# A two-layer decoder trunk in float32: the MLP's down projection as Strassen products

## The chip, the cores and the metric

The kernel runs on one core of a Trainium2 chip. The metric is the device time of one execution in microseconds (us). Times are medians of several executions. The engines of a core work side by side, each through its own queue in order: TensorE (matmuls; PE in the profile, its weight loads PEld), VectorE (DVE), ScalarE (ACT), GpSimd (POOL) and SyncE (SP, which issues most DMAs).

## The reference

`x` is [1, 256, 2048] in float32: 256 tokens. Two layers follow each other. Each has a mixer (several kinds of attention between an input and an output projection) and an MLP; the change touches the MLP. In float32:

```python
def squared_relu_mlp(h, w_up, w_down):
    return jnp.square(jax.nn.relu(h @ w_up)) @ w_down

for layer in range(2):
    ...
    h = rms_norm(x, mlp_norm[layer])
    x = x + squared_relu_mlp(h, w_up[layer], w_down[layer])
return rms_norm(x, final_norm)
```

`w_up` is [2048, 8192] and `w_down` [8192, 2048] for each layer.

## The kernel before

**Three passes.** A float32 product is made of three matmul passes in the type float32r. Weights and activations are split into a high and a low part, w = wh + wl and x = xh + xl, and wh·xh + wh·xl + wl·xh is summed in PSUM. Activations lie feature-major; a moving operand is the tile [xh | xl] of 512 columns.

**The weight stream.** All projections form one list, `stream`, of (block, chunk). A `Block` is 256 output columns of a projection; a `Chunk` is four K-tiles of it (4 x 128 rows x 256 columns). A `Unit` is one load, usually 4 K-tiles x 512 columns (1 MB), which serves one chunk of each of two blocks (`pair` weaves the two). The main loop goes through the list. For chunk i it issues, in this order: ScalarE's copy of the high part (`hi_to`, line 1077) up to chunk i+4; VectorE's subtraction for the low part (`lo_to`, line 1085) up to chunk i+3; the matmuls of chunk i (`consume`); and then `jobs.tick()`. There are three raw buffers, five for hi and four for lo. A raw buffer is loaded anew once the last chunk of its load has its low part.

**The kinds of a block.** "T" (lines 445 to 448): for each K-tile and each of two column tiles, a matmul of the high weights over 512 columns [xh | xl] and one of the low weights over 256 columns (xh). "N" (lines 434 to 436): the activations are stationary and the weights move, three matmuls of 256 columns. "last" (lines 440 to 442): three matmuls of 256 columns with the weights stationary; only the last 256 columns of the last layer are of this kind.

**Side work.** Norms, splits and attention are generators in `Jobs`. `tick` runs those that are due; a `yield d, pe` puts the next step off by d ticks. What a step issues stands in the engines' queues behind what the loop has issued by then.

**The MLP.** The hidden 8192 columns go in two groups of 4096. For each group the up projection runs (16 blocks of 16 K-tiles), its results are squared and split into h (`up_done`, lines 933 to 946), and then the down projection over these 4096 rows (8 blocks of 32 K-tiles), whose results are scaled by the norm and added to the residual xT (`down_done`). The order of the blocks is written out by hand.

Of the kernel before, what the change touches and what calls it, by code (L numbers as in the profile page):

```python
# [38 lines left out]
class Jobs:  # L39
    """Side work (attention, norms, splits) that is woven between the weight chunks."""  # L40
# [48 lines left out]
class Ring:  # L89
    """Order of use of the buffers of one tag: a buffer is free once its key is done."""  # L90
# [13 lines left out]
class Unit:  # L104
    """One load: up to 4 K-tiles x 512 columns of a weight, for one or two chunks."""
# [5 lines left out]
class Chunk:  # L111
    """Some K-tiles of a block: views(raw) are the parts of the load in the order of the operand."""

    def __init__(self, unit, kts, views):
        self.unit, self.kts, self.views = unit, kts, views
        unit.users += 1


class Block:
    """256 output columns of one projection (128 where tiles is 1)."""  # L120

    def __init__(self, kind, chunks, mov, done, tiles=2):
        self.kind, self.chunks, self.mov, self.done, self.tiles = kind, chunks, mov, done, tiles
        self.total = sum(len(c.kts) for c in chunks)
        self.count, self.ps = 0, None
# [3 lines left out]
def trunk(ctx, tc, x, attn_norm, mlp_norm, w_up, w_down, ev_w_in, ev_q_norm, ev_w_uq, ev_kv_norm,  # L129
# [5 lines left out]
    psum = ctx.enter_context(tc.tile_pool(name="psum", bufs=1, space=bass.MemoryType.PSUM))  # L135
    ctx.enter_context(tc.manual_schedule())
# [48 lines left out]
    # the tensor engine's clock rises while the first loads are under way  # L185
    def keep_warm(n):
        if "warm" not in st:
            st["warm"] = psum.tile([P, 2, 512], F32, name="mm", bufs=3)[:, 0]
# [22 lines left out]
    def make_xs(b, g0):  # L211
        """Next phase's moving operand from residual block b, and its sum of squares."""
# [19 lines left out]
    def sum_squares(acc, ms, size):  # L232
        """ms [P, 2] <- mean square + eps per token, tokens on partitions."""
# [5 lines left out]
    def broadcast(r, rB):  # L239
        """rB [P, T] <- r [P, 2] along the free axis, on every partition."""  # L240
# [46 lines left out]
    def w_chunks(w, c0, groups, width=512):  # L287
        """Loads of K-tile groups x width columns of w [K, N]: the chunks of each 256 columns."""
# [23 lines left out]
    def evac(ps, dst, scale=None, rB=None):  # L312
        """dst [P, 2, T] <- sum of the bank halves, times scale, times rB along tokens."""
# [11 lines left out]
    def scores(pairs, dist, cs, u):  # L325
        """u [P, 2, 384] <- biased logits of two heads: [q0 k0 | q1 k0 | q1 k1]."""
# [9 lines left out]
    def neg_max(u, nm):  # L336
        """nm [P, 2 (q tile), 2 (head)] <- -max."""
# [13 lines left out]
    def transpose_p(u):  # L351
        """In place: [k0 q0 | k0 q1 | k1 q1]."""
# [55 lines left out]
    stream = []  # L408

# [4 lines left out]
    def consume(block, i, hi, lo):  # L414
        if block.ps is None:
            block.ps = psum.tile([P, 2, 512], F32, name="mm", bufs=3)
            if block.kind == "last":
                block.ps = [block.ps[:, 0, 0:T], psum.tile([P, 2, 512], F32, name="mm", bufs=3)[:, 0, 0:T]]
# [9 lines left out]
        for n, j in order:  # L428
# [10 lines left out]
            if block.kind == "last":  # L439
# [14 lines left out]
    def even_mixer():  # L454
# [5 lines left out]
        def open_pool():  # L460
            pool = E["pool"] = pool_ctx.enter_context(tc.tile_pool(name="even", bufs=1, reuse_waits="tile"))
# [78 lines left out]
        # the shared rotary key, on both partition halves  # L540
# [11 lines left out]
        def rotate(src, n, outs):  # L552
            """outs <- src*cos + swap(src)*sin; src [P, n, T]."""
# [29 lines left out]
        # per-head projections  # L583
# [38 lines left out]
        def cut(view, pr, width, a, b):  # L622
            """The columns a:b of the two heads, width columns each, of a load."""
# [68 lines left out]
        # output projection  # L692
# [18 lines left out]
    def odd_mixer():  # L711
# [7 lines left out]
        def open_pool():  # L719
            pool = E["pool"] = pool_ctx.enter_context(tc.tile_pool(name="odd", bufs=1, reuse_waits="tile"))  # L720
# [78 lines left out]
        # dilated groups: slots 2*sp, 2*sp+1 of the three groups, one joint softmax  # L799
# [112 lines left out]
    def mlp(layer, last):  # L912
# [6 lines left out]
        def open_pool():  # L919
# [316 lines left out]
```

## Time and profile before

| | us |
|---|---|
| median of 3 runs | 2188.74 (2188.19 to 2188.99) |
| span of the profiled execution, first to last instruction | 2186.0 |
| TensorE busy | 2173.6 |
| VectorE busy | 1298.6 |
| ScalarE busy | 1022.6 |

The span is counted from the first to the last instruction of one profiled execution. Its whole time has 2 to 3 us around the span, as the runs show beside it. Busy times of TensorE overlap, since a matmul begins before the one ahead has drained; prices are read from one start to the next.

### The profile page before, as it was taken

The numbers are of one execution on the slowest core, as the hardware profiler recorded it, in microseconds if no ns is written. First come the engines' busy times: TensorE is split into PE (matmuls) and PEld (weight loads), VectorE is DVE, ScalarE is ACT, GpSimd is POOL, SyncE is SP. The second block draws the span as 40 slices with busy tenths as digits, with TensorE's granted clock in tenths as the row PEclk, the third lists the DMA queues.
The fourth block names the chain that finished last, engine by engine and source line by source line (L and its number), as shares of the span: only waits on it lengthen the run. The fifth ranks groups of instructions, "written<-read, shape, count | busy, mean of one in ns | idle before, by whom it ended". The sixth has DMA issues, their size and how long they took to land.

```text
span 2186.0 us, 31244 instructions
## 1 busy us (share of the span) xinstructions
PE 2173.6 (99%) x12902; PEld 1917.1 (88%) x12902; DVE 1298.6 (59%) x1576; ACT 1022.6 (47%) x1377; POOL 12.8 (1%) x24
## 2 busy tenths in 40 slices
PE   9999999999999999999999999999999999999998
PEld 7898988888888888888888889988888888888887
DVE  6766666656545565556667665566565556655554
ACT  6554544444434444444445446444443334444443
POOL 0000000000000000000000000000000000000000
PEclk9999999999999999999999999999999999999999
DMA  8544455555555555655654456665555555555544
GB/s 260 182 149 155 147 188 184 184 194 175 198 187 192 191 182 187 207 190 176 188 166 148 154 174 190 158 193 184 186 183 199 185 184 189 192 185 183 191 154 135
DMA packets 211374, 396.26 MB, mean 181 GB/s; under 512 B 8904, under 2 KB 31504, under 8 KB 211104
## 3 DMA queue, kind: packets, MB, share of 16 engines
q1 hardware_dynamic: 210720, 392.33, 55.3%
q8 instruction: 101, 1.65, 0.3%
q0 software_dynamic: 480, 1.94, 0.3%
q14 instruction: 41, 0.34, 0.0%
q10 hardware_dynamic: 32, 0.01, 0.0%
HBM read 392.15 MB, written 2.10 MB: 180 GB/s over the span
## 4 chain that ended last, share of the span: by engine, by line
PE 99%; DMA 0%; ACT 0%; SPq 0%; DVE 0%; POOLq 0%; issue 0%; ACTq 0%; DVEq 0%
PE mm L445 55%; PE mm L446 30%; PE mm L448 3%; PE mm L435 2%; PE mm L434 2%; PE mm L436 2%; PE side L333 1%; PE side L356 1%; PE side L402 1%; PE side L331 1%; PE mm L442 0%; PE mm L440 0%; PE mm L441 0%; PE side L403 0%; DMA latqs<-ev_w_in 0%; PE side L873 0%
## 5 line engine op out<-in xcount | busy, mean ns | idle before, releaser
L1085 DVE TENSOR_TENSOR lo<-raw,hi 128x1024 fp32r<-128x1024 f32 (+1 forms) x756 | 898.6, 1194 | 627.2 <-PE mm L446 555.4
L1077 ACT ACTIVATE hi<-raw 128x1024 fp32r<-128x1024 f32 (+1 forms) x756 | 780.6, 1036 | 804.9 <-PE mm L445 712.4
L445 PE MATMUL mm<-xs,hi 128*128 128x512 f32 x2805 | 995.3, 396 | 0.5 <-ACT hi L1077 0.3
L446 PE MATMUL mm<-xs,lo 128*128 128x256 f32 x2992 | 820.5, 279 | 0.2 <-DVE lo L1085 0.2
L445 PE MATMUL mm<-h,hi 128*128 128x512 f32 x1922 | 675.0, 393 | 0.0
L445 PEld LDWEIGHTS mm<-xs,hi 128*128 128x128 f32 x2805 | 526.0, 188 | 121.1 <-ACT hi L1077 1.0
L446 PEld LDWEIGHTS mm<-xs,lo 128*128 128x128 f32 x2992 | 561.4, 188 | 8.8 <-DVE lo L1085 0.5
L446 PE MATMUL mm<-h,lo 128*128 128x256 f32 x1984 | 548.7, 279 | 0.0
L445 PEld LDWEIGHTS mm<-h,hi 128*128 128x128 f32 x1922 | 360.2, 187 | 84.4
L446 PEld LDWEIGHTS mm<-h,lo 128*128 128x128 f32 x1984 | 371.9, 187 | 2.8
L434 PE MATMUL mm<-hi,xs 128*128 128x256 f32 x320 | 91.8, 287 | 0.0
L936 DVE TENSOR_TENSOR t<-mm,t 128x512 f32<-128x512 f32 x64 | 44.3, 691 | 77.3 <-ACT t L935 77.3
L436 PE MATMUL mm<-hi,xs 128*128 128x256 f32 x320 | 89.7, 280 | 0.0
L435 PE MATMUL mm<-lo,xs 128*128 128x256 f32 x320 | 89.7, 280 | 0.0
L935 ACT ACTIVATE t<-mm 128x512 f32<-128x512 f32 x64 | 38.3, 598 | 100.3 <-PE mm L448 100.3
L448 PE MATMUL mm<-xs,hi 128*128 128x512 f32 x187 | 69.9, 396 | 0.0
L445 PE MATMUL mm<-oT,hi 128*128 128x512 f32 x192 | 67.6, 394 | 0.0
L435 PEld LDWEIGHTS mm<-lo,xs 128*128 128x128 f32 x320 | 60.3, 188 | 0.2
L434 PEld LDWEIGHTS mm<-hi,xs 128*128 128x128 f32 x320 | 60.3, 188 | 0.2
L436 PEld LDWEIGHTS mm<-hi,xs 128*128 128x128 f32 x320 | 60.2, 188 | 0.0
L446 PE MATMUL mm<-oT,lo 128*128 128x256 f32 x192 | 53.6, 279 | 0.0
L315 ACT ACTIVATE t<-mm 128x512 f32<-128x512 f32 x37 | 22.1, 598 | 53.8 <-PE mm L448 53.8
(266 smaller groups left out, 1494.3 us busy)
## 6 DMA issues: line engine op xcount, KB each, us to landing
raw<-w_up SPq DMA_DIRECT2D x128, 1024.0 KB, 5.3
raw<-w_down SPq DMA_DIRECT2D x120, 1024.0 KB, 5.0
raw<-od_w_in SPq DMA_DIRECT2D x36, 1024.0 KB, 5.1
raw<-ev_w_in SPq DMA_DIRECT2D x30, 1024.0 KB, 5.4
raw<-ev_w_out SPq DMA_DIRECT2D x16, 1024.0 KB, 5.0
raw<-od_w_in SPq DMA_DIRECT2D x20, 512.0 KB, 4.1
raw<-od_w_out SPq DMA_DIRECT2D x16, 512.0 KB, 6.0
raw<-w_down SPq DMA_DIRECT2D x16, 512.0 KB, 3.6
```

Of the source, the lines that this page charges most:

```text
L315: act(t, ps[:, :, T:], AF.Copy, scale=1.0 if scale is None else scale)
L331: mm(ps[:, 0:P], q[:, 0:P], k[:, 0:P], start=(i == 0), stop=(i == n - 1))
L434: mm(o, xh, hi[:, n], start=first, stop=False)
L435: mm(o, xh, lo[:, n], start=False, stop=False)
L436: mm(o, xl, hi[:, n], start=False, stop=last)
L445: mm(ps[:, j], hi[:, n, c], m, start=first, stop=False)
L446: mm(ps[:, j, 0:T], lo[:, n, c], m[:, 0:T], start=False, stop=False)
L448: mm(ps[:, j], hi[:, n, c], m, start=False, stop=True)
L935: act(t, ps[:, :, T:], AF.Copy)
L936: tt(t, ps[:, :, 0:T], t, op=OP.add)
L1077: act(d, r, AF.Copy)
L1085: tt(d, r, f32(h), op=OP.subtract)
```

## The change

The MLP's hidden columns go in eight groups of 1024. The first seven groups' down projection is made of Strassen products (the form with seven products, and sums shared between them). A 2 x 2 block here is two token halves (128 tokens) by two K-tiles on the activations' side, and two K-tiles by two halves of 512 columns on the weights' side. The activations are stationary (seven combinations of 128 tokens, high and low part), the weights move (256 columns).

- `up_done` evacuates with a relu and a square on ScalarE; its job makes four sums on VectorE and the seven combinations, split into high and low, in `hs` (eight buffers of seven combinations).
- The weights of one load give four chunks: products 1 and 2 (unchanged weights), 3 (unchanged), 5 and 7 (a first set of differences, `prep13`), 6 and 4 (a second set, `prep24`). VectorE makes the differences, ahead of the hi copies.
- The seven product sums of a column block of 512 lie in PSUM tiles s0 and s1 (two banks each) over one group. ScalarE copies them to a stage tile, and a POOL DMA adds them to a DRAM tensor (the first group writes it).
- Behind the seventh group `combine` reads the seven sums back, adds them on VectorE, scales by the norm on ScalarE, and transposes on TensorE into the residual.
- The products of a group are woven with the up projection of the next: two product chunks, one up chunk. Up blocks are of the new kind "U" (three matmuls of 256 columns, both passes of the high weights into the same PSUM columns), one bank each, two buffers. Up loads and the last group's down loads are 8 K-tiles x 256 columns.
- The last group's down projection stays "T" (and "last"), over 8 K-tiles. A residual block is finished once `combine` and this block have both added to it.
- PSUM tiles for blocks come from a pool that each phase opens anew. Comments are taken out; the lines stay in place.

```diff
+        mm(ps[:, j], hi[:, n, c], m[:, 0:T], ...)      # kind "U"
+        mm(ps[:, j], hi[:, n, c], m[:, T:], ...)
+        mm(ps[:, j], lo[:, n, c], m[:, 0:T], ...)
...
+    def consume_products(block, i, hi, lo):
+        chunk = block.chunks[i]
...
+        for o, (a, prod) in enumerate(chunk.prods):
+            half, at = HOME[prod]
+            if half not in block.ps:
+                block.ps[half] = banks(half, 1)
+            ps = block.ps[half].rearrange("p b c -> p (b c)")[:, at * T:(at + 1) * T]
+            for q, pr in enumerate(chunk.kts):
+                x = block.mov(pr)
+                first, last = block.count < 4 and q == 0, block.count >= block.total - 4 and q == 1
+                mm(ps, x[:, a, 0:P], hi[:, o, q], start=first and at % 2 == 0, stop=False)
+                mm(ps, x[:, a, 0:P], lo[:, o, q], start=False, stop=False)
+                mm(ps, x[:, a, P:], hi[:, o, q], start=False, stop=last and (at % 2 == 1 or prod == 3))
+        block.count += 1
+        if block.count == block.total - 2:
+            block.done("s0", block.ps["s0"])
+        if block.count == block.total:
+            block.done("s1", block.ps["s1"])
...
-        NGRP = 2
+        NGRP = 8
...
         def up_done(grp, b):
             def f(ps):
-                r = E["pool"].tile([P, 2, T], F32, name="hr", bufs=3)
                 t = temp()
-                act(t, ps[:, :, T:], AF.Copy)
-                tt(t, ps[:, :, 0:T], t, op=OP.add)
-                stt(r, t, 0.0, t, op0=OP.max, op1=OP.mult)
+                act(t, ps, AF.Relu)
+                r = E["pool"].tile([P, 8, P], F32, name="hr", bufs=1)
+                act(r[:, 0:4].rearrange("p (j k) t -> p j (k t)", j=2), t, AF.Square)
 
                 def job():
-                    h = hs[grp, b] = E["pool"].tile([P, 2, 2 * T], F32R, name=f"h{b}")
-                    split_into(h, r)
+                    h = E["pool"].tile([P, 7, 2 * P], F32R, name="hs", bufs=2 * nb)
+                    if grp == NGRP - 1:
+                        h = h.rearrange("p o t -> p (o t)")[:, 0:4 * T].rearrange("p (j t) -> p j t", j=2)
+                        split_into(h, r[:, 0:4].rearrange("p (j k) t -> p j (k t)", j=2))
+                    else:
+                        tt(r[:, 4], r[:, 0], r[:, 2], op=OP.add)
+                        tt(r[:, 6], r[:, 1], r[:, 0], op=OP.subtract)
+                        tt(r[:, 5], r[:, 4], r[:, 1], op=OP.subtract)
+                        tt(r[:, 7], r[:, 3], r[:, 5], op=OP.subtract)
+                        act(h[:, :, 0:P], r[:, 1:8], AF.Copy)
+                        tt(h[:, :, P:], r[:, 1:8], f32(h[:, :, 0:P]), op=OP.subtract)
+                    hs[grp, b] = h
...
+                def prep13(unit=unit, made=made):
+                    w = blocks(unit.raw)
+                    t = made[13] = E["pool"].tile([P, 1024], F32, name="w13")
+                    tt(four(t), w[:, :, :, 1].rearrange("p q k c -> p k q c"),
+                       w[:, :, 0].rearrange("p q h c -> p h q c"), op=OP.subtract)
+                def prep24(unit=unit, made=made):
+                    w = blocks(unit.raw)
+                    t = made[24] = E["pool"].tile([P, 1024], F32, name="w24")
+                    tt(four(t)[:, 0], four(made[13])[:, 1], w[:, :, 0, 0], op=OP.add)
+                    tt(four(t)[:, 1], w[:, :, 1, 0], four(t)[:, 0], op=OP.subtract)
...
+                chunks += [Chunk(unit, ks, plain, prods=((X11, 1), (X12, 2))),
+                           Chunk(unit, ks, single, prods=((S4, 3),)),
+                           Chunk(unit, ks, of(13), prep13, ((S1, 5), (S3, 7))),
+                           Chunk(unit, ks, of(24), prep24, ((S2, 6), (X22, 4)))]
...
+        def products_done(grp, cb):
+            def f(half, ps):
+                n = 3 if half == "s0" else 4
+                stage = E["pool"].tile([P, 4 * T], F32, name="stage", bufs=2)[:, 0:n * T]
+                act(stage, ps.rearrange("p b c -> p (b c)")[:, 0:n * T], AF.Copy)
+                to = sums[cb][:, 0:n * T] if half == "s0" else sums[cb][:, 3 * T:]
+                if grp == 0:
+                    nc.gpsimd.dma_start(to, stage)
+                else:
+                    nc.gpsimd.dma_start(to, stage, accum_op=OP.add)
+                if grp == NGRP - 2 and half == "s1":
+                    jobs.spawn(combine(cb), keys=[("sum", cb)], delay=1)
+            return f
+
+        def combine(cb):
+            s = E["pool"].tile([P, 7, 2 * P], F32, name="hs", bufs=2 * nb)
+            nc.gpsimd.dma_start(s, sums[cb].rearrange("p (o c) -> p o c", o=7))
+            yield 3, 0
+            p1, p2, p3, p5, p7, p6, p4 = (s[:, i] for i in range(7))
+            g = E["pool"].tile([P, 2, 2, T], F32, name="hr", bufs=1)
+            u2, u43 = temp(), temp()
+            tt(u2[:, 0], p1, p6, op=OP.add)
+            tt(g[:, 1, 0], p1, p2, op=OP.add)
+            tt(u43, u2[:, 0:1].to_broadcast([P, 2, T]), s[:, 3:5], op=OP.add)
+            tt(g[:, 1, 1], u43[:, 0], p3, op=OP.add)
+            tt(g[:, 0, 0], u43[:, 1], p4, op=OP.add)
+            tt(g[:, 0, 1], u43[:, 1], p5, op=OP.add)
+            r = E.setdefault("r", st["r"])
+            for tok in range(2):
+                act(g[:, tok], g[:, tok], AF.Copy, scale=r[:, tok:tok + 1])
+            yield 1, 1
+            for i in range(2):
+                b = 2 * cb + i
+                ps = side().rearrange("p (j t) -> p j t", j=2)
+                for j in range(2):
+                    for tok in range(2):
+                        nc.tensor.transpose(ps[:, j, tok * P:(tok + 1) * P], g[:, tok, i, j * P:(j + 1) * P], ident)
+                tt(xT[b], xT[b], ps, op=OP.add)
+                if i == 0:
+                    yield 1, 1
...
+        stream.extend(up_list(0))
+        for grp in range(NGRP - 1):
+            s, u = product_list(grp), up_list(grp + 1)
+            for i in range(len(u)):
+                stream.extend(s[2 * i:2 * i + 2] + u[i:i + 1])
...
+            prep = stream[i][0].chunks[stream[i][1]].prep
+            if prep:
+                prep()
...
-        if block.tiles * len(block.chunks[c].kts) == 8:
+        if block.tiles * len(block.chunks[c].kts) == 8 or block.kind == "S" and c % 2:
             jobs.tick()
```

## Rows read from the trace of the kernel before

**Rows 1.** The page: span, busy times (share, instructions), chain by line.
```profile
span 2186.0 us, 31244 instructions
...
PE 2173.6 (99%) x12902; PEld 1917.1 (88%) x12902; DVE 1298.6 (59%) x1576; ACT 1022.6 (47%) x1377; POOL 12.8 (1%) x24
...
PE mm L445 55%; PE mm L446 30%; PE mm L448 3%; PE mm L435 2%; PE mm L434 2%; PE mm L436 2%; PE side L333 1%; PE side L356 1%; PE side L402 1%; PE side L331 1%; PE mm L442 0%; PE mm L440 0%; PE mm L441 0%; PE side L403 0%; DMA latqs<-ev_w_in 0%; PE side L873 0%
```

**Rows 2.** The waits: who waited for whom, us, times, longest.
```profile
ACT hi L1077 <- PE mm L445: 712.4, 421, 3.1
DVE lo L1085 <- PE mm L446: 555.4, 387, 2.8
...
PE mm L446 <- DVE lo L1085: 0.2, 1, 0.2
```

**Rows 3.** Timeline of TensorE, three stretches: start us, us, engine, line, what.
```profile
1000.20 0.39 PE L445 MATMUL mm<-h,hi 128*128 128x512 f32 x1
...
1009.30 0.39 PE L445 MATMUL mm<-h,hi 128*128 128x512 f32 x1
...
1365.93 0.28 PE L434 MATMUL mm<-hi,xs 128*128 128x256 f32 x1
...
1370.86 0.28 PE L434 MATMUL mm<-hi,xs 128*128 128x256 f32 x1
...
2156.68 0.29 PE L440 MATMUL mm<-h,hi 128*128 128x256 f32 x1
...
2161.72 0.29 PE L440 MATMUL mm<-h,hi 128*128 128x256 f32 x1
```

**Rows 4.** The chain that ended last: four transposes at the end.
```profile
2156.06 0.44 PE side L999 x4
```

**Rows 5.** Windows in these stretches: busy us and count by engine, clock, DMA.
```profile
2156.60:2172.60 16.00, 16.00 (x136) 16.00 (x135) 4.44 (x5) 2.12 (x2) 0.00 (x0) 1.00 0.14 43
1366.00:1376.00 10.00, 10.00 (x87) 10.00 (x87) 4.27 (x4) 4.40 (x6) 0.00 (x0) 1.00 0.64 184
1000.00:1010.00 10.00, 10.00 (x60) 8.69 (x58) 4.50 (x5) 4.16 (x4) 0.00 (x0) 1.00 0.72 233
```

**Rows 6.** Groups of VectorE by shape: busy us, mean ns, idle before.
```profile
L1085 DVE TENSOR_TENSOR lo<-raw,hi 128x1024 fp32r<-128x1024 f32 x716 | 872.8, 1222 | 614.1 <-PE mm L446 551.0 <-PE mm L435 36.2 <-issue 18.8
...
L1085 DVE TENSOR_TENSOR lo<-raw,hi 128x512 fp32r<-128x512 f32 x40 | 25.8, 686 | 13.1 <-issue 7.1 <-PE mm L446 4.4 <-PE mm L435 1.6
...
L560 DVE TENSOR_TENSOR t<-side,rope 128x256 f32<-128x256 f32 x5 | 2.1, 419 | 1.6 <-PE side L556 1.6
```

**Rows 7.** Timeline of VectorE: a run of three lo, and dependent operations.
```profile
34.84 3.50 DVE L1085 TENSOR_TENSOR lo<-raw,hi 128x1024 fp32r<-128x1024 f32 x3
...
718.29 0.69 DVE L952 TENSOR_TENSOR t<-mm,t 128x512 f32<-128x512 f32 x1 [2.16 <-ACT t L951]
719.02 0.69 DVE L954 TENSOR_TENSOR t<-t,rB 128x512 f32<-128x512 f32 x1
```

**Rows 8.** Groups of ScalarE by shape.
```profile
L1077 ACT ACTIVATE hi<-raw 128x1024 fp32r<-128x1024 f32 x716 | 757.4, 1059 | 788.0 <-PE mm L445 700.4 <-issue 25.2 <-DMA raw<-w_down 17.5
...
L935 ACT ACTIVATE t<-mm 128x512 f32<-128x512 f32 x64 | 38.3, 598 | 100.3 <-PE mm L448 100.3
```

**Rows 9.** DMA issues: count, KB each, median us from issue to landing.
```profile
raw<-w_up SPq DMA_DIRECT2D x128, 1024.0 KB, 5.3
...
raw<-w_down SPq DMA_DIRECT2D x16, 512.0 KB, 3.6
...
fn<-final_norm POOLq DMA_DIRECT2D x1, 1024.0 KB, 5.7
odist<-c_dist POOLq DMA_DIRECT2D x1, 768.0 KB, 6.8
...
sk<-od_sinks POOLq DMA_DIRECT2D x1, 8.0 KB, 2.8
```

**Rows 10.** Window of the landing of sk, columns as in rows 5.
```profile
1038.80:1041.60 2.80, 2.80 (x18) 2.44 (x17) 2.80 (x6) 2.17 (x3) 1.45 (x5) 1.00 0.18 15
```

More of the change, by code (lines that the diff above doesn't have):

```diff
@@ L111, with __init__ @@
 class Chunk:
-    def __init__(self, unit, kts, views):
-        self.unit, self.kts, self.views = unit, kts, views
+    def __init__(self, unit, kts, views, prep=None, prods=()):
+        self.unit, self.kts, self.views, self.prep, self.prods = unit, kts, views, prep, prods
         unit.users += 1
 class Block:
-    def __init__(self, kind, chunks, mov, done, tiles=2):
+    def __init__(self, kind, chunks, mov, done, tiles=2, take=None):
         self.kind, self.chunks, self.mov, self.done, self.tiles = kind, chunks, mov, done, tiles
-        self.total = sum(len(c.kts) for c in chunks)
+        self.total = len(chunks) if kind == "S" else sum(len(c.kts) for c in chunks)
+        self.take = take
         self.count, self.ps = 0, None
@@ L408, in trunk @@
     stream = []
+    X11, X22, X12, S1, S2, S3, S4 = range(7)
+    HOME = {1: ("s0", 0), 2: ("s0", 1), 3: ("s0", 2), 5: ("s1", 0), 7: ("s1", 1), 6: ("s1", 2), 4: ("s1", 3)}
     def add(block):
@@ L414, in consume @@
     def consume(block, i, hi, lo):
+        if block.kind == "S":
+            return consume_products(block, i, hi, lo)
         if block.ps is None:
-            block.ps = psum.tile([P, 2, 512], F32, name="mm", bufs=3)
-            if block.kind == "last":
-                block.ps = [block.ps[:, 0, 0:T], psum.tile([P, 2, 512], F32, name="mm", bufs=3)[:, 0, 0:T]]
+            block.ps = (block.take or banks)()
         ps, tiles, kts = block.ps, block.tiles, block.chunks[i].kts
@@ L438, in consume @@
             c = slice(j * P, (j + 1) * P)
-            if block.kind == "last":
+            if block.kind == "U":
+                mm(ps[:, j], hi[:, n, c], m[:, 0:T], start=first and j == 0, stop=False)
+                mm(ps[:, j], hi[:, n, c], m[:, T:], start=False, stop=False)
+                mm(ps[:, j], lo[:, n, c], m[:, 0:T], start=False, stop=last and j == 1)
+            elif block.kind == "last":
                 mm(ps[j], hi[:, n, c], m[:, 0:T], start=first, stop=False)
@@ new lines, in combine @@
+        def combine(cb):
[24 more added lines that the diff above has]
+                    yield 1, 1
+            jobs.done.add(("sum", cb))
+            for b in (2 * cb, 2 * cb + 1):
+                finish(b)
@@ L948, in f, with finish, down_done @@
+        left = [2] * 8
+        def finish(b):
+            left[b] -= 1
+            if left[b] == 0:
+                if last:
+                    final_block(E, b)
+                else:
+                    x_done(b, g_next, 2)
+        def down_done(b):
             def f(ps):
@@ new lines, in f, with eights, load, views @@
+                finish(b)
+            return f
+        def eights(w, c0, n):
+            view = w.rearrange("(k p) c -> p k c", p=P)
+            chunks = []
+            for a in range(0, n, 8):
+                def load(raw, a=a):
+                    nc.sync.dma_start(raw.rearrange("p (k c) -> p k c", c=T), view[:, a:a + 8, c0:c0 + T])
+                unit = Unit(load)
+                for h in range(2):
+                    def views(raw, dst, h=h):
+                        return [(dst, raw[:, h * 1024:(h + 1) * 1024])]
+                    chunks.append(Chunk(unit, list(range(a + 4 * h, a + 4 * h + 4)), views))
+            return chunks
@@ new lines, in up_list, with product_list, mov @@
+        def up_list(grp):
+            blocks = [Block("U", eights(up, grp * W + b * T, KT), mov, up_done(grp, b), take=take_up)
+                      for b in range(nb)]
+            return [(block, i) for block in blocks for i in range(len(block.chunks))]
+        def product_list(grp):
+            def mov(pr):
+                need(("h", layer, grp, pr))
+                return hs[grp, pr]
+            blocks = [Block("S", product_chunks(down[grp * W:(grp + 1) * W], cb * 512), mov, products_done(grp, cb))
+                      for cb in range(4)]
+            return [(block, i) for block in blocks for i in range(len(block.chunks))]
@@ new lines, in mlp, with h_mov @@
+        stream.extend(up_list(0))
[3 more added lines that the diff above has]
+                stream.extend(s[2 * i:2 * i + 2] + u[i:i + 1])
+        def h_mov(kt):
+            need(("h", layer, NGRP - 1, kt // 2))
+            return hs[NGRP - 1, kt // 2][:, kt % 2]
+        wd = down[FF - W:]
+        for b in range(8):
+            if last and b == 7:
+                add(Block("last", eights(wd, b * T, W // P), h_mov, lambda ps: last_block(E, ps), take=take_last))
+            else:
+                add(Block("T", eights(wd, b * T, W // P), h_mov, down_done(b), take=take_down(b)))
@@ L1013, in last_block @@
             act(sq[:, j], xl[:, j], AF.Square)
-        sums, turn = psum.tile([P, 2, 512], F32, name="mm", bufs=3), side()
+        sums, turn = banks("s1", 1), side()
         def add_up(a, first, last):
```

69 lines of the change are left out of this document (44 added, 25 removed).

## The prediction

> **What bounds the kernel now.** I read the page first: the span, the busy share of each engine and the chain that ended last. The reader is to see that TensorE is busy for nearly the whole span and that the chain is almost all matmuls of the weight stream (lines 445 and 446) [rows 1]. Then the waits: ScalarE (hi) and VectorE (lo) wait for TensorE to release their buffers, hundreds of us in all, and TensorE waits for them next to nothing [rows 2]. So in the MLP a change is worth what it does to TensorE's time, as long as VectorE, ScalarE and the loads stay ahead. The third view is the timeline of TensorE at three stretches, because the change alters the shape of the matmuls and the busy time overlaps: only start to start is a price [rows 3]. From first and last row of each:
> - a "T" pair (one 512-column and one 256-column matmul): 26 pairs from 1000.20 to 1009.30, 0.350 us;
> - an "N" triple (three of 256 columns; activations stationary, weights moving): 14 from 1365.93 to 1370.86, 0.352 us;
> - a "last" triple (three of 256; weights stationary): 14 from 2156.68 to 2161.72, 0.360 us.
>
> The clock granted is 1.00 in all three, and weight loads fill the N and last stretches [rows 5].
>
> **TensorE, before against after.** One layer's MLP is 1024 (K-tile, column-tile) steps up and 1024 down. Before, they are pairs, but for 64 last triples of layer 1: 4032 x 0.350 + 64 x 0.360 = 1434.2 us. After:
> - Up: kind "U" issues the instructions of "last" (hi·xh, hi·xl, lo·xh): 2048 x 0.360 = 737.3. This part is a loss of 20.5.
> - Down, seven of eight groups: each load (4 K-tiles x 512 columns) gives 7 products x 2 halves of K = 14 triples; 2 loads x 4 column blocks x 7 groups x 2 layers = 112 loads, 1568 triples. Each is an N triple (xh, xh, xl stationary; hi, lo, hi of the weights moving): x 0.352 = 551.9, where the pairs it replaces (2 x 896) cost 627.2.
> - Down, last group: 240 pairs and 16 last triples, 89.8.
>
> Sum 1379.0: 55.2 less. `combine` adds 8 blocks x 8 transposes; four take 0.44 us on the chain [rows 4], so +7.0. Net -48.2.
>
> What a 256-column matmul costs decides this, so one rule is weighed. The row says 0.117 to 0.120 us for each matmul of a triple and 0.350 for a pair [rows 3]. The Trainium skill, "TensorE: Matmul & The Clock Gate", section "Back-to-back issue gap", puts the isolated gap at the columns over 2.4 GHz plus about 2.5 ns, which makes a pair 0.325 and a triple 0.328. By it the same counts would save some 63 us instead of 55; the trace does not agree with it here, being 7 to 8% dearer, and the rows are used.
>
> **VectorE in the woven stretch.** The order is two chunks of products, one chunk U, and so on. A double cycle has two loads of products (28 triples) and four U chunks (32): 9.86 + 11.52 = 21.4 us of TensorE. There are 56 of them. VectorE's operations cost 1.22, 0.69 and 0.42 us at 1024, 512 and 256 elements [rows 6]; independent ones follow each other after 1.14 (three in 3.50), a dependent one of 512 after 0.73 [rows 7]. So full-size ones cost 1.14, those of 512 0.60, dependent 0.73. For the double cycle: ten lo and two prep13 at 1.14 = 13.7; two lo of 512 at 0.60 = 1.2; two prep24 at 0.60 + 0.73 = 2.7; together 17.5. One block of h: four operations of 128 elements (0.2 to 0.3 by the step from 512 to 256), the wait for ScalarE's copy of 896 (about 1.0, just under hi's 1.06 [rows 8]), the subtraction of 896 (1.0): 3.05. Sum 20.6 us of 21.4, 96%. ScalarE: ten hi at 1.06, two at 0.62 (a 512-element copy is about 0.60), 0.6 + 0.6 for relu and square, 1.0 for the copy, about 2.0 for two stage copies: some 16 us, 75%.
>
> VectorE is thus nearly as long as TensorE, and its queue is in order. I followed it by hand through one double cycle: lo of chunk i+3 cannot start before TensorE has released chunk i-1, and the h job of a finished block stands between the lo of the next cycle's fourth product chunk and that of its second U chunk. That last lo is the tightest place: done about 0.5 us before TensorE wants it. Everywhere else one to three us remain, and the queue stands at the cycle's end as it stood at its start. I take 0.1 us of wait per double cycle, 5 us in all. Bounds: 0 (it keeps up) and about 60 (VectorE 5% over TensorE, 1.07 x 56).
>
> Loads: 2 MB per 10.7 us is no more than now (1 MB in 5.6). U's loads have rows of 1 KB; the nearest row, 512 KB in 3.6 us, adds at its own rate to some 5.5 for 1 MB, beside 5.3 now [rows 9]. From the release of a raw buffer to its first hi lie about 6 to 7 us: taken as hidden, with its failure inside the 60.
>
> **The sums in DRAM.** POOL issues 112 transfers (384 or 512 KB: two for each of 4 blocks, 7 groups, 2 layers), of which 96 accumulate; nothing waits for them until the stage buffer comes round, 21 us later. But `combine` is on the path: TensorE itself queues behind it, since its transposes are issued a fixed number of ticks after the read. From the end of a block's last product chunk TensorE has one U chunk and one cycle (2.9 + 10.7 = 13.6 us) before the transposes. The chain: stage copy 1.1, accumulation of 512 KB, read of 896 KB, six vector operations 2.5, two scalings 1.2. No row shows an accumulation: below it is bounded by the 3.6 us of a plain 512 KB load, above by twice that; I take 4.5, nearer the plain one. The read lies between 5.0 (fn, 1 MB in 5.7, scaled) and odist's 6.8; 5.5 taken [rows 9]. Sum 14.8 (13.4 to 18.9): a wait of 1.2 (0 to 5.3) for the first two column blocks. The third's read takes the ninth and later `hs` tile in order, whose buffer still holds h of group 6 until TensorE has done the fourth block's first four chunks, 7.8 us into the cycle: 7.8 + 5.5 + 3.7 = 17.0 against 10.7, a wait of 6.3 (5.8 to 7.6). The fourth has 2.9 + 4 x 2.8 = 14.1 of cover: 0.7 (0 to 4.8). Per layer 9.4, in all 19 (12 to 46). While VectorE waits for the read, the lo behind it are late too; TensorE holds three, so the transposes stop it first.
>
> **Edges.** Last group: its second chunk needs the h just made (relu 0.6, square 0.6, a hi 1.06, split 0.6, subtraction 0.7 = 3.6 against 2.8), 0.8 twice. Its eight down blocks have only two chunks each (5.6 us), and VectorE has two lo, three evacuations, next operand and squares, about 5.9: the lead of some 8 us goes, and next phase or tail starts about 2.5 late, twice. Together 7 (0 to 15).
>
> The span of 2186.0 lies 2.7 below the runs' median of 2188.7; the sum is made on the latter, as what lies around the span is not touched: 2188.7 - 48.2 + 5 + 19 + 7 = 2171.5 us.
>
> **Rivals.**
> 1. VectorE becomes the bound. For: 96%, a margin of 0.5 us. Against: the hand count closes, and ScalarE has a quarter free. Place: lo of the U chunk behind h. At 5% over: 2171.5 - 5 + 60 = 2226. It decides from 22 us in all, 0.39 per double cycle, which makes the time what it was. This is the one on the other side.
> 2. The sums' transfers are slow beside the loads. For: odist's 768 KB took 6.8 [rows 9]. At its upper bound 2171.5 - 19 + 46 = 2198; it decides from 36, 4.5 us per block.
> 3. POOL's transfers starve while VectorE is busy, each held for a run of three lo, 3.5 us [rows 7]. Two stand in each of eight combines: 2171.5 + 56 = 2227. Against: a POOL transfer of 8 KB landed in 2.8 us [rows 9] while VectorE was busy for all 2.80 us [rows 10]. [...]
> 4. The products don't get the N price: new outputs alternate inside banks, and if a triple takes 0.400, 1568 x 0.048 = 75 goes, 2247, slower. For: no row shows outputs alternating so; against: N has the same operands and its two outputs alternate too, in two banks.
>
> **Chances.** Forecast 0.64 (own range 2145 to 2185), rival 1 0.15, rival 2 0.13, rival 3 0.03, rival 4 0.05. The measurement tells about 0.2% (4.4 us) from no change. Faster: 0.59 of the forecast, 0.02 and 0.03 of rivals 1 and 2: 0.64. Same: 0.04, 0.02, 0.03: 0.09. Slower: 0.27. All waits at their lower bounds give 2188.7 - 48.2 + 12 = 2152; if U's triples went at the N price, 16 less; the range begins between, at 2145, and reaches past rival 2 to a mild rival 1, 2210; about 0.05 lie below and 0.13 above.
>
> **What would show it.** Right: TensorE starts 0.35 apart per triple, waits on lo of a few tenths, PE busy near 99%, four visible waits at the transposes of each layer, the third the longest, VectorE above 90% busy in the woven stretch. Wrong: TensorE waiting for lo in each double cycle; ScalarE waiting on raw or on stage; triples above 0.36; the accumulations landing after 8 us or more.

## The result, and the profile after

The changed kernel takes 2224.94 us (median of 4 runs, 2223.32 to 2231.32) against 2188.52 before: ratio 1.0172, 95% interval 1.0157 to 1.0186. It is 36 us slower; 17 faster was forecast, and the time lies above the range.

The page of the changed kernel, to be read beside [rows 1]: span, busy times, granted clock by slice.

```profile
span 2221.5 us, 39419 instructions
...
PE 2156.0 (97%) x16086; PEld 2058.3 (93%) x16086; DVE 1745.0 (79%) x2248; ACT 1316.7 (59%) x1777; POOL 108.9 (5%) x144
...
PEclk9999999999999999999999999999999999999898
```

TensorE's busy time fell by 17.6 us and its share from 99 to 97%: some 65 us of the span are now not matmuls, where 12 were. The second view is that of the waits, against [rows 2]: who waited for whom, us, times, longest.

```profile
ACT hi L1276 <- DMA raw<-w_up: 169.2, 80, 5.5
...
DVE hs L1016 <- ACT hs L1015: 60.5, 56, 1.1
...
ACT hr L1098 <- DVE hr L1095: 46.2, 8, 7.8
...
PE side L1105 <- ACT hr L1098: 43.1, 9, 7.6
...
DVE t L1090 <- DMA hs<-sums: 39.4, 8, 7.5
...
PE up L465 <- DVE lo L1284: 6.2, 13, 1.6
```

Read from below: TensorE waits for lo only 6.2 us, but 43.1 at the transposes of `combine` (L1105), there for ScalarE's scaling (L1098), that for VectorE's sums (L1095), and these for the read of the sums (L1090). It is one chain, eight times. The first two rows are new too: ScalarE waits for U's loads, and VectorE for ScalarE's copy in each h job.

The DMA view gives the chain's transfers (count, KB, median us from issue to landing), against [rows 9]:

```profile
raw<-w_up SPq DMA_DIRECT2D x128, 1024.0 KB, 5.8
raw<-w_down SPq DMA_DIRECT2D x128, 1024.0 KB, 6.4
...
sums<-stage POOLq DMA_DIRECT2D x56, 512.0 KB, 6.1
sums<-stage POOLq DMA_DIRECT2D x56, 384.0 KB, 6.4
...
hs<-sums POOLq DMA_DIRECT2D x8, 896.0 KB, 7.4
```

Now the first combine of layer 0 on the timelines (start us, us, engine, line, what). ScalarE:

```profile
949.72 1.06 ACT L1276 ACTIVATE hi<-raw 128x1024 fp32r<-128x1024 f32 x1 [1.37 <-DVE lo L1284]
950.68 1.01 ACT L1072 ACTIVATE stage<-s 128x1024 f32<-128x1024 f32 x1
...
969.04 1.33 ACT L1098 ACTIVATE hr<-hr,r 128x512 f32<-128x512 f32 x2 [6.14 <-DVE hr L1095]
```

GpSimd (its issues):

```profile
951.98 0.86 POOL L1077 DMA_DIRECT2D sums<-stage  x1 [3.94 <-ACT stage L1072]
958.76 0.57 POOL L1085 DMA_DIRECT2D hs<-sums  x1 [5.92 <-PE s L498]
```

VectorE:

```profile
956.84 2.96 DVE L1284 TENSOR_TENSOR lo<-raw,hi 128x1024 fp32r<-128x1024 f32 x3
966.46 0.42 DVE L1090 TENSOR_TENSOR t<-hs 128x256 f32<-128x256 f32 x1 [6.66 <-DMA hs<-sums]
...
968.53 0.42 DVE L1095 TENSOR_TENSOR hr<-t,hs 128x256 f32<-128x256 f32 x1
```

TensorE:

```profile
949.09 0.28 PE L498 MATMUL s<-hi,hs 128*128 128x256 f32 x1
949.20 0.28 PE L463 MATMUL up<-xs,hi 128*128 128x256 f32 x1
...
962.70 0.28 PE L465 MATMUL up<-xs,lo 128*128 128x256 f32 x1
969.82 1.52 PE L1105 MATMUL side<-misc,hr 128*128 128x128 f32 x4 [6.84 <-ACT hr L1098]
```

The column block's last product ends at 949.20, and TensorE reaches the transposes behind 962.70: a cover of 13.5 us, as counted (13.6). But the chain runs to 969.82, 20.6 us instead of 14.8. It has these pieces:

| piece | us | counted |
|---|---|---|
| the stage copy waits behind a hi on ScalarE | 1.5 | 0 |
| stage copy, until GpSimd issues | 1.3 | 1.1 |
| accumulation, until the read is issued | 6.8 | 4.5 |
| read, until VectorE starts | 7.7 | 5.5 |
| six vector operations | 2.6 | 2.5 |
| scaling, until the first transpose | 0.8 | 1.2 |

VectorE stands idle for 6.66 us of it, with the lo of the coming chunks behind it. The windows around this wait (us, then busy us and count of PE, PEld, DVE, ACT and POOL, granted clock, DMA share, GB/s) show two more things:

```profile
956.00:962.70 6.70, 6.70 (x58) 6.70 (x57) 3.57 (x4) 2.64 (x4) 0.57 (x1) 1.00 1.02 331
962.70:969.80 7.10, 0.28 (x3) 0.07 (x1) 3.31 (x7) 0.96 (x3) 0.00 (x0) 0.85 0.34 136
969.80:974.00 4.20, 4.04 (x18) 3.75 (x19) 4.01 (x6) 2.04 (x3) 0.00 (x0) 0.50 0.02 4
```

The DMA engines are full while the accumulation ends and the read begins, and nearly empty behind it: no raw buffer comes free while VectorE waits. And TensorE, idle for 6.84 us, comes back at half clock (0.50, the 1.2 GHz level): the four transposes take 1.52 us, where four took 0.44 [rows 4]. The clock is only a part of that, as the run with more cover will show.

### The profile page after: what moved, and what is told of

Read it like the earlier page. It is cut to its first block, busy times and chain, and to the rows that moved or that the text cites. A ratio compares the mean times of both kernels' runs of the same rounds, so it can differ in the third digit from the quotient of the medians.

```text
span 2221.5 us, 39419 instructions
## 1 busy us (share of the span) xinstructions
PE 2156.0 (97%) x16086; PEld 2058.3 (93%) x16086; DVE 1745.0 (79%) x2248; ACT 1316.7 (59%) x1777; POOL 108.9 (5%) x144
## 4 chain that ended last, share of the span: by engine, by line
issue 26%; PE 20%; DMA 2%; POOL 2%; DVE 2%; ACT 1%; POOLq 0%; ACTq 0%; DVEq 0%; SPq 0%
PE mm L472 7%; PE mm L473 4%; POOL sums L1077 2%; PE mm L457 1%; PE mm L458 1%; PE mm L459 1%; DMA sums<-stage 1%; DMA hs<-sums 1%; PE up L463 1%; PE up L464 1%; PE up L465 1%; DVE lo L1284 1%; PE side L350 1%; DMA raw<-w_up 1%; PE mm L475 1%
## 5 line engine op out<-in xcount | busy, mean ns | idle before, releaser
L465 PE MATMUL up<-xs,lo 128*128 128x256 f32 x2048 | 579.6, 283 | 6.6 <-DVE lo L1284 6.2
L463 PE MATMUL up<-xs,hi 128*128 128x256 f32 x2048 | 578.8, 283 | 1.6 <-DVE xT L757 1.6
L464 PE MATMUL up<-xs,hi 128*128 128x256 f32 x2048 | 579.0, 283 | 0.0
L496 PE MATMUL s<-hi,hs 128*128 128x256 f32 x1568 | 445.7, 284 | 0.0
L497 PE MATMUL s<-lo,hs 128*128 128x256 f32 x1568 | 444.1, 283 | 0.0
L498 PE MATMUL s<-hi,hs 128*128 128x256 f32 x1568 | 443.7, 283 | 0.0
L465 PEld LDWEIGHTS up<-xs,lo 128*128 128x128 f32 x2048 | 387.8, 189 | 12.0 <-DVE lo L1284 11.2
L463 PEld LDWEIGHTS up<-xs,hi 128*128 128x128 f32 x2048 | 385.2, 188 | 1.9 <-ACT hi L1276 1.9
L464 PEld LDWEIGHTS up<-xs,hi 128*128 128x128 f32 x2048 | 385.0, 188 | 0.0
L472 PE MATMUL mm<-xs,hi 128*128 128x512 f32 x885 | 319.5, 401 | 0.4 <-ACT hi L1276 0.4
L496 PEld LDWEIGHTS s<-hi,hs 128*128 128x128 f32 x1568 | 300.1, 191 | 0.0
L498 PEld LDWEIGHTS s<-hi,hs 128*128 128x128 f32 x1568 | 299.5, 191 | 0.0
L1284 DVE TENSOR_TENSOR lo<-w,hi 128x1024 fp32r<-128x1024 f32 x224 | 273.8, 1222 | 24.2 <-ACT hi L1276 18.9
L473 PE MATMUL mm<-xs,lo 128*128 128x256 f32 x944 | 259.3, 280 | 0.2 <-DVE lo L1284 0.2
L473 PEld LDWEIGHTS mm<-xs,lo 128*128 128x128 f32 x944 | 177.5, 188 | 3.0 <-DVE lo L1284 0.5
```

Of the source, the lines that this page charges most:

```text
L463: mm(ps[:, j], hi[:, n, c], m[:, 0:T], start=first and j == 0, stop=False)
L464: mm(ps[:, j], hi[:, n, c], m[:, T:], start=False, stop=False)
L465: mm(ps[:, j], lo[:, n, c], m[:, 0:T], start=False, stop=last and j == 1)
L472: mm(ps[:, j], hi[:, n, c], m, start=first, stop=False)
L473: mm(ps[:, j, 0:T], lo[:, n, c], m[:, 0:T], start=False, stop=False)
L496: mm(ps, x[:, a, 0:P], hi[:, o, q], start=first and at % 2 == 0, stop=False)
```

## The experiments

All ratios are to the kernel before, measured beside each run (medians from 2188.2 to 2188.7, so that the runs can be held against each other); "the changed kernel" is at 2224.9.

**What the combines cost in all.** The body of `combine` is left out.

```diff
-            s = E["pool"].tile([P, 7, 2 * P], F32, name="hs", bufs=2 * nb)
-            nc.gpsimd.dma_start(s, sums[cb].rearrange("p (o c) -> p o c", o=7))
             yield 3, 0
-            p1, p2, p3, p5, p7, p6, p4 = (s[:, i] for i in range(7))
...
+            yield 1, 0
+            yield 1, 0
```

> The body of the combine is left out (no read of the sums, no additions, no transposes), so that the seven groups' share of the down projection is missing from the result; the ticks stay. It gives the price of all combines together. Theory A: 44 us of waits, 15 of lower clock and 7 of transposes go, 2225 falls to 2155 to 2163, and the woven stretch keeps its length of about 602 us from the first U matmul of layer 0 to the place of its first transposes. Theory B: less than 20 us go, above 2205.

2164.31 us, 0.9895 (0.9879 to 0.9912). The eight combines cost 60.6 us; the prediction had 26 (19 of waits, 7 of transposes). What is left without them still lies just above the expectation.

**What the adding costs.** Each group writes over the sums instead of adding to them.

```diff
-                    nc.gpsimd.dma_start(to, stage, accum_op=OP.add)
+                    nc.gpsimd.dma_start(to, stage)
```

> The stage tiles are written to DRAM plainly instead of being added there, so that the sums hold the last group alone. It tells what the adding itself costs. Theory A: a plain write of 512 KB lands 1 to 2.5 us earlier than the 6.1 us of the accumulating one, each of the eight chains gets that much shorter, and the time falls by 8 to 20 us, to 2205 to 2217. Rival: the 6.1 us come from the loads beside it and not from the adding; the landing stays at 6 us and the time within 5 us of 2225.

2202.68 us, 1.0065 (1.005 to 1.008). The DMA view of this run:

```profile
sums<-stage POOLq DMA_DIRECT2D x56, 512.0 KB, 3.6
sums<-stage POOLq DMA_DIRECT2D x56, 384.0 KB, 3.6
hs<-sums POOLq DMA_DIRECT2D x8, 896.0 KB, 6.4
```

A plain write of 512 KB lands in 3.6 us, the same as the plain load of [rows 9]; adding takes 2.5 more. With 3.5 us less in the chain (the read is 1.0 shorter too), the wait at the transposes goes from 43.1 to 23.8 us in this run's waits, and the time falls by 22, more than expected. The rival, that the 6.1 us come from the loads beside it, is out.

**More cover.** `combine` issues its vector operations and transposes seven ticks behind the read instead of three; nothing is left out.

```diff
-            yield 3, 0
+            yield 7, 0
```

> The combine of a column block issues its sums seven ticks after the read of DRAM instead of three; nothing else changes. Four ticks more are one U chunk and one and a half product chunks for each two, 10.7 us of TensorE in the woven stretch. Theory A (44 us of waits at the first transposes, which are 3.8 to 7.7 us each, and some 15 us of lower granted clock behind them): all waits vanish, 2225 falls to 2166 to 2176, the price of the kernel without combine (2164) and the transposes (7). Theory B (the work of the combine itself on VectorE is what costs, and would be paid at the U chunks instead): above 2195.

2186.23 us, 0.9994 (0.9984 to 1.0003): 38.7 less than the changed kernel, and level with the kernel before. In its waits:

```profile
PE side L1105 <- ACT hr L1098: 9.3, 14, 2.3
PE up L465 <- DVE lo L1284: 8.0, 19, 1.2
PE s L472 <- DVE hs L166: 3.1, 2, 1.6
```

The chain theory is right for most of the loss, but the time stops between the two expectations: something else costs TensorE too. A longer delay has no time: with nine ticks, expected at 2165 to 2175, the program deadlocks; why is not known.

This run also shows what the half clock costs. From the first transposes of layer 0 on, at the granted clock of 1.00, it starts 32 matmuls in 4.2 us (the first four on the timeline, then the window, columns as above):

```profile
977.23 0.33 PE L1105 MATMUL side<-misc,hr 128*128 128x128 f32 x1 [0.24 <-ACT hr L1098]
977.84 0.55 PE L1105 MATMUL side<-misc,hr 128*128 128x128 f32 x3 [0.29 <-ACT hr L1098]
```

```profile
977.20:981.40 4.20, 3.89 (x32) 3.70 (x33) 4.17 (x6) 2.38 (x4) 0.00 (x0) 1.00 1.05 266
```

In the changed kernel it was 18, at 0.50. (The four transposes take 1.16 us here at full clock, with a wait for ScalarE's second scaling inside them; of the 1.52 us the clock made some 0.4.) In all eight stretches at half clock 104 matmuls of the weight stream begin; by their starts in the trace they take 25.2 us, where as many at full clock take 13.5: some 12 us (an estimate).

**The lower clock.** Fourteen matmuls that nothing reads (3.3 us) stand before the first transposes, three ticks kept.

```diff
             yield 1, 1
+            fill = side()
+            for _ in range(14):
+                mm(fill, xs_all[:, 0, 0:P], xs_all[:, 0], start=True, stop=True)
```

> Before the first transposes of each combine TensorE gets 14 matmuls of 512 columns whose result nobody reads (3.3 us at 0.233), so that most of each wait of 3.8 to 7.7 us is spent on matmuls; three ticks as in the changed kernel. It tells the wait from the lower clock behind it. If the lower granted clock of 3.4 to 10.2 us behind each wait costs about 2 us each and comes from TensorE standing, the time falls by 5 to 15 us, to 2210 to 2220, and the clock's rows stay nearer 1. If the loss behind each wait has another cause (late lo, the second transposes), the time is 2225 within 4 us, or above it.

2226.65 us, 1.0176 (1.0161 to 1.0191): nothing gained, as the second expectation had it. That does not make the half clock free. The wait at the transposes fell to 19.1, but the filling takes its own time, and it had to wait once, in the fourth block of layer 0, for the operand that it reads:

```profile
PE side L1102 <- DVE xs L234: 6.2, 1, 6.2
```

19.1 + 6.2 + 8 x 3.3 = 51.7 us of waits and filling stand where 43.1 us of waits were. That is 8.6 more, and the time rose by 1.7: some 7 us came back (an estimate) as the mean clock of the profiled run rose from 0.987 to 0.993.

**Has VectorE slack?** `prep13` is made twice, 1.2 us more in each of 112 loads.

```diff
                     tt(four(t), w[:, :, :, 1].rearrange("p q k c -> p k q c"),
                        w[:, :, 0].rearrange("p q h c -> p h q c"), op=OP.subtract)
+                    tt(four(t), w[:, :, :, 1].rearrange("p q k c -> p k q c"),
+                       w[:, :, 0].rearrange("p q h c -> p h q c"), op=OP.subtract)
```

> Each first set of weight differences is made twice (the second time over the first), 1.14 us more of VectorE for each load of products, 2.3 us for a double cycle of 21.4 us; the result is unchanged. If VectorE was at 96 per cent as counted, it is now 1.5 us or more over TensorE, becomes the bound of the woven stretch, and adds 1.4 to 2.3 us to each of 56 double cycles: 2225 rises by 80 to 130 us, to 2305 to 2355. If VectorE had real slack in the woven stretch, the time stays within 20 us of 2225.

2319.55 us, 1.0594 (1.0579 to 1.061): 94.6 more, for 112 x 1.22 = 136.6 us of added work. In its waits TensorE now stops for lo:

```profile
PE up L465 <- DVE lo L1286: 71.9, 48, 2.0
```

So there is little slack: 42 us of the added work were absorbed, 0.75 per double cycle. The timeline of VectorE in the changed kernel shows why, from one h job (L1011) to the next, one double cycle:

```profile
653.91 0.28 DVE L1011 TENSOR_TENSOR hr<-hr 128x128 f32<-128x128 f32 x1
...
656.00 1.09 DVE L1016 TENSOR_TENSOR hs<-hr,hs 128x896 fp32r<-128x896 f32 x1 [1.08 <-ACT hs L1015]
657.01 2.96 DVE L1284 TENSOR_TENSOR lo<-raw,hi 128x1024 fp32r<-128x1024 f32 x3
...
667.37 1.83 DVE L1284 TENSOR_TENSOR lo<-raw,hi 128x1024 fp32r<-128x1024 f32 x2 [0.23 <-ACT hi L1276]
...
674.30 1.23 DVE L1284 TENSOR_TENSOR lo<-w,hi 128x1024 fp32r<-128x1024 f32 x1 [0.27 <-ACT hi L1276]
675.44 0.28 DVE L1011 TENSOR_TENSOR hr<-hr 128x128 f32<-128x128 f32 x1
```

The double cycle takes 21.53 us, and VectorE works in nearly all of it; its idle time is the 1.08 for ScalarE's copy (which the prediction had counted) and twice a quarter of a us before a lo whose hi was not there. These two are about the 0.5 us of margin that the prediction had: it is there in the sum, and whether it is there where a lo is due, the runs without `prep24` tell.

**The price of U.** The kernel before, with its up projection alone in the new kind.

```diff
...
-            pair(*(Block("T", c[i], mov, up_done(grp, b + i)) for i in range(2)))
+            pair(*(Block("U", c[i], mov, up_done(grp, b + i)) for i in range(2)))
```

> The kernel before with its up projections alone as three matmuls of 256 columns (relu and square on ScalarE, both high passes into the same PSUM columns); loads, groups and down projection stay. By the rows of before a triple is 0.360 us and a pair 0.350: 2048 x 0.010 = 20 us more, 2188.7 becomes 2205 to 2213. Rival: the triple is bound by its third weight load and costs 0.40 or more in long runs, above 2270; or nothing, 2189.

2207.14 us, 1.0086 (1.007 to 1.0103): 18.9 more, 20.5 in the prediction. This term stands.

**Less work on VectorE, with the cover.** Seven ticks, and `prep24` left out (2.65 us per double cycle).

```diff
-                            Chunk(unit, ks, of(24), prep24, ((S2, 6), (X22, 4)))]
+                            Chunk(unit, ks, of(13), None, ((S2, 6), (X22, 4)))]
```

> Seven ticks as in the run beside it, and the second set of weight differences is left out (products 6 and 4 take the first set, so the result is not the reference's): 2.65 us less VectorE for each double cycle of 21.4 us. It tells what VectorE's lateness still costs in the woven stretch. If the waits of U's lo (4.9 us in layer 0) and their like are VectorE's, the time is 5 to 12 us below the run beside it; if the woven stretch's surplus over the count is the matmuls' own price, it is the same within 4 us.

2165.88 us, 0.99 (0.9885 to 0.9915): 20.3 below the seven ticks alone, more than the 5 to 12 of the theory, and far from the rival's 4. VectorE's lateness is the second cost: work that the sum has room for is paid all the same.

**Neither.** No combine (as above) and no `prep24`: what is left is TensorE, if the matmuls were priced rightly.

> The changed kernel without the body of combine (no read of the sums, no vector sums, no transposes) and without the second set of weight differences (prep24; the products that used it take the first set), so the output is not the reference's. It measures what is left of the woven stretch when neither the combines nor VectorE's load are there. Lateness of VectorE: the prices of the matmuls give 2188.7 - 55.2 = 2133.5, the edges of the prediction 7 more, 2140; 2138 to 2150 is expected, 14 to 26 below the kernel without combine (2164.3). Rival (matmuls that are dearer than counted, or edges that have nothing to do with VectorE): 2158 to 2166.

2140.94 us, 0.9783 (0.9768 to 0.9797): inside the theory's range. In this run TensorE waits nowhere for lo but once (0.2 us), and ScalarE's wait for `w_up` falls from 169 to 49. The 23.4 us between this and the kernel without combine are thus VectorE's, by itself and by the raw buffers that it frees late: in the waits of the run without combine stand

```profile
PE up L465 <- DVE lo L1262: 8.2, 15, 1.5
PE s L472 <- DVE hs L166: 3.6, 2, 2.2
```

which name half of it. By the trace, from the first product triple to the last the two woven stretches take 607.6 and 604.7 us without combine, 598.2 and 597.8 with neither: 16 of the 23.4 us are lost there. The other 7 lie behind them, in the last group, the next phase and the tail.

**The h job split.** Without combine, and with the h job's subtraction (L1016) one tick later, so that no lo stands behind its wait for ScalarE.

```diff
                         act(h[:, :, 0:P], r[:, 1:8], AF.Copy)
+                        yield 1, 0
                         tt(h[:, :, P:], r[:, 1:8], f32(h[:, :, 0:P]), op=OP.subtract)
```

> The changed kernel without the body of combine, and with the h job's last subtraction one tick later, so that the lo queued behind it do not stand behind ScalarE's copy; the output is not the reference's. If the h job's wait for ScalarE is what makes VectorE late in the woven stretch: 2155 to 2160, 4 to 9 below the kernel without combine (2164.3). If that wait is absorbed when no combine disturbs: within 2 of 2164.

2162.4 us (2156.45 to 2166.83), 0.9872 (0.9855 to 0.9888): within 2 of the kernel without combine, and the runs spread over 10 us. By this run the 1.08 us don't pay where nothing else disturbs; the spread leaves it open.

The same edit with the combines at seven ticks, nothing left out:

> Seven ticks in combine as before, and the h job's last subtraction is issued one tick later than the copy it waits for, so that VectorE makes a lo in place of waiting 1.1 us for ScalarE in each of 56 double cycles (60 us of waiting in the trace). The result is the same. Theory: VectorE's lateness costs the 20 us that went when its second set of differences was left out (2.65 us a double cycle); 1.1 us a double cycle gives back much of it: 2168 to 2180, below the kernel before. Rival: only the amount of VectorE's work counts, not where it waits, since it waits when it is ahead anyway: 2183 to 2190.

2180.73 us (2176.42 to 2183.99), 0.9963 (0.9949 to 0.9978): 5.5 below the seven ticks alone, just above the theory's range and below the rival's, and the one kernel here that does the whole work and is faster than before, by 0.37%.

**The first set on GpSimd.** Seven ticks, `prep13` on the engine with 5% of work.

```diff
-                    tt(four(t), w[:, :, :, 1].rearrange("p q k c -> p k q c"),
+                    nc.gpsimd.tensor_tensor(four(t), w[:, :, :, 1].rearrange("p q k c -> p k q c"),
```

> Seven ticks, and GpSimd makes the first set of weight differences instead of VectorE (112 operations of 1024 elements), 2.3 us less VectorE for each double cycle. The result is the same. Theory: if GpSimd takes under some 4 us for one and does not hold up VectorE, the 20 us come back: 2164 to 2172. Rival (the shared port, or GpSimd's queue, in which a transfer of the sums waits for ScalarE ahead of it): VectorE's own operations get longer or the differences come too late, and the time is above 2190.

2464.86 us, 1.1256 (1.124 to 1.1272). The groups of this run by shape, VectorE and GpSimd (busy us, mean ns, idle before):

```profile
L1284 DVE TENSOR_TENSOR lo<-raw,hi 128x1024 fp32r<-128x1024 f32 x604 | 738.2, 1232 | 252.8 <-PE up L465 80.9 <-PE mm L473 70.4 <-PE mm L458 36.2
L1284 DVE TENSOR_TENSOR lo<-w,hi 128x1024 fp32r<-128x1024 f32 x224 | 363.0, 1621 | 57.5 <-ACT hi L1276 36.2 <-PE up L465 17.2
```

```profile
L1043 POOL TENSOR_TENSOR w<-raw 128x1024 f32<-128x1024 f32 x112 | 286.4, 2558 | 629.6 <-DMA raw<-w_down 469.6 <-DVE lo L1284 159.9
L1077 POOL DMA_DIRECT2D sums<-stage x96 | 83.6, 871 | 846.7 <-ACT stage L1072 647.9 <-DVE lo L1284 184.2 <-ACT hi L1276 14.7
```

GpSimd takes 2.56 us where VectorE takes 1.22, and VectorE's lo on the differences take 1.62 instead of 1.22 in the mean. By the times in the trace, 57 of these 224 lo overlap one of GpSimd's subtractions and take 2.79 in the mean; the other 167 take 1.22. The Trainium skill, "SBUF — State Buffer", section "SBUF: two separate sides", says that GpSimd and VectorE share a pair of ports which one instruction holds to its end while the other waits, where VectorE's has two inputs in SBUF and GpSimd's reads SBUF; these stretched lo agree with it.

They add some 90 us of VectorE's time, and the kernel lost 279 against seven ticks alone. The other half of the rival is in the trace too: in GpSimd's queue 89 of the 112 subtractions start right behind the issue of a transfer of the sums, which waits for its stage copy (here done at 673.84), and VectorE waits for the difference:

```profile
672.81 1.03 ACT L1072 ACTIVATE stage<-s 128x1024 f32<-128x1024 f32 x1 [0.36 <-PE s L498]
674.13 0.86 POOL L1077 DMA_DIRECT2D sums<-stage  x1 [4.76 <-DVE lo L1284]
674.70 2.73 POOL L1043 TENSOR_TENSOR w<-raw 128x1024 f32<-128x1024 f32 x1
677.46 0.69 DVE L1049 TENSOR_TENSOR w<-w,raw 128x512 f32<-128x512 f32 x1 [3.48 <-POOL w L1043]
```

How the loss is shared between the ports, the slower subtraction and the queue was not tested.

With the h job split as well:

> Both edits of the two runs beside it. Theory: VectorE has then 3.4 us to spare in each double cycle, and the time is at the floor of this schedule, 2162 to 2170. Rival: as for the first set on GpSimd, above 2190.

2350.09 us, 1.0734 (1.0719 to 1.0749): better by 115, and still far from either kernel.

## Why the prediction was wrong

The whole error, 2224.9 - 2171.5 = 53.4 us, can be shared among the terms of the sum by three runs: 2140.9 with neither combine nor `prep24`, 2164.3 without combine, 2224.9.

| term | predicted | measured | off by |
|---|---|---|---|
| matmuls | -55.2 | 2140.9 - 2188.7 = -47.8 | 7.4 |
| VectorE: woven stretch 5, edges 7 | +12 | 2164.3 - 2140.9 = +23.4 | 11.4 |
| combine: waits 19, transposes 7 | +26 | 2224.9 - 2164.3 = +60.6 | 34.6 |

- **The step that failed is the combine term.** Its mechanism was stated and is right: TensorE queues behind the read of the sums, with 13.5 us of cover. The size was 19 (12 to 46) and is 53.6 beside the 7 of transposes, above the upper bound; 43.1 of it show as waits. The accumulation was taken at 4.5, "nearer the plain one", and landed in 6.1, inside its bounds; the read was taken at 5.5 (bound 6.8) and took 7.4, outside; the 1.5 us on ScalarE's queue and the time to the issue were left out. Five to six us in the chain cost over 30 because the counted chain was already 1.2 us longer than the cover: past that point each us is paid eight times. The plain write agrees in size: 3.5 us less in the chain took 19 off the waits and 22 off the time. And one cost was put at nothing without a reason: the half clock behind each wait, some 12 us by the starts above.
- **The two special cases failed.** In layer 0 the third wait was the shortest and not the longest, since its read went out 0.6 us after the accumulation had landed and was not held by the `hs` buffer, and the fourth was no 0.7. TensorE's timeline has them:

```profile
1028.76 0.33 PE L1105 MATMUL side<-misc,hr 128*128 128x128 f32 x1 [3.65 <-ACT hr L1098]
...
1058.28 1.52 PE L1105 MATMUL side<-misc,hr 128*128 128x128 f32 x4 [4.51 <-ACT hr L1098]
```

- **VectorE.** Rival 1 held in part. The count of its work (20.6, the wait for the copy included) was 0.4 short of the 21.0 us that VectorE needs in the double cycle above. That leaves the 0.5 us of margin in the sum, but not at each lo: the woven stretches lost 16 us where 5 were counted, and behind them some 7 were lost, as the edges had it. The rival's price of 60 was far off. The falsifier "ScalarE waiting on raw" came true with it (169 us, and 49 with neither).
- **Matmuls.** The mechanism was right. U measured +18.9 for +20.5. The product triples start 0.356 us apart in the mean over all 1568 in the run with neither, not 0.352: 6 of the 7.4 us. The rest can be edges, which that run still holds. By the gap formula of the Trainium skill, "TensorE: Matmul & The Clock Gate", section "Back-to-back issue gap", weighed in the prediction, the saving would have been some 63; the trace's 0.356 is near the row's 0.352 and not near the formula's 0.328. (The "last" triple, whose 0.360 prices U, is 10% dearer than the formula's, not 7 to 8.)
- **The rivals.** Rival 2 (slow sums, 2198) was the right place at too low a price: its bound was made from single transfers and did not have the queues between them. Rival 3 (starving issues) did not happen: with VectorE 91% busy (328.93 of 360 us from 600 to 960), an issue took 0.86 us and the accumulation landed in 6.1, and without the adding in 3.6, the time of the plain load. Rival 4 did not happen. That 2224.9 lies beside the prices of rival 1 (2226) and rival 3 (2227) is chance: rival 3's path was not taken, and rival 1's gave 23 of its 60.
- **The load of U** was put at 5.5 us from a row of 512 KB in 3.6, which at that row's rate gives 7.2 and not 5.5; it measured 5.8.
- **Open.** The 60.6 us add up as an estimate: 43.1 of waits, some 10 of transposes (by their starts in the run with seven ticks, 1.27 us a block), 12 of half clock, less the 5.6 by which the waits for lo and hs are shorter than without combine (6.2 for 8.2 + 3.6). No run has the waits without the half clock behind them. With seven ticks and no `prep24` the time is still 25 above the run with neither; by the trace some 19 of it lie behind the last product triples of the layers, where the late combines end, and what they wait for there was not taken apart.

## What to carry to other kernels

When a change puts a round trip through DRAM on the path of the bottleneck engine, sum the whole chain with its queues (the copy that waits its turn, the issue, the landing under full loads, the engine that must take the result) and hold it against the cover in the issue order; if they are within a few us, move the consumer later before anything else, as this one line (three ticks to seven) was worth 38.7 us here. When an engine's count comes to 96% of the bottleneck's, treat it as one that will be late: double one of its operations and leave one out, and see whether the time follows. A margin in the sum does not say that each operation is there when it is due.

## What the hardware showed that was not expected

- An accumulating DMA of 512 KB into DRAM landed in 6.1 us, a plain one in 3.6; the two sizes of 384 and 512 KB took the same (6.4 and 6.1; 3.6 and 3.6).
- At waits of 3.7 to 7.6 us TensorE's granted clock went to half (1.2 GHz) for 3.4 to 10.2 us, eight times in this kernel; the first of them came behind some 600 us of U and product matmuls at 1.00. Product matmuls start 0.119 us apart at full clock and some 0.21 at half.
- GpSimd's subtraction of 1024 elements took 2.56 us, and a lo of VectorE that overlapped one took 2.79 in the mean instead of 1.22.
